# A float32 decoder trunk on one core: the FFN's last down group of three pairs by token block, the embedding's gate by token block, and other places for the first loads and the rotary tables

## The chip, the cores and the metric

The kernel runs on one core of a Trainium2 chip. The metric is the device time of the whole program in microseconds, as a median of several runs. The program computes two decoder layers on 512 tokens of 1024 features, all in float32. The core has five engines with queues of their own: TensorE (PE in the profile; its weight loads are PEld), VectorE (DVE), ScalarE (ACT), GpSimd (POOL) and SyncE (SP), which here issues the DMAs. Engines wait for each other by semaphores. Each engine takes its instructions in the order that was fixed when the program was built.

## The reference

Each layer runs four sub-layers, every one normalised before and after: a feed-forward network (FFN) at half weight, a token mixer, a second FFN, and a gated embedding. The mixer is retention with rotary positions in layer 0 and stick-breaking attention in layer 1.

```python
def swiglu(x, w_gate, w_up, w_down):
    return (jax.nn.silu(x @ w_gate) * (x @ w_up)) @ w_down

for i in range(DEPTH):
    g = norm_gains[i]
    f = swiglu(rmsnorm(h, g[0]), ffn_w_gate[i, 0], ffn_w_up[i, 0], ffn_w_down[i, 0])
    h = h + FFN_RES_WEIGHT * rmsnorm(f, g[1])
    m_in = rmsnorm(h, g[2])
    j = i // N_MIXERS
    if i % N_MIXERS == 0:
        m = retention(m_in, positions, ret_w_in[j], ret_gn_gain[j], ret_w_out[j])
    else:
        m = stick_breaking(m_in, sb_w_in[j], sb_w_out[j])
    h = h + rmsnorm(m, g[3])
    f = swiglu(rmsnorm(h, g[4]), ffn_w_gate[i, 1], ffn_w_up[i, 1], ffn_w_down[i, 1])
    h = h + FFN_RES_WEIGHT * rmsnorm(f, g[5])
    gate = jax.nn.sigmoid(rmsnorm(h, g[6]) @ ple_w_gate[i])
    e = p[i] @ ple_w_proj[i]
    h = h + rmsnorm(gate * e, g[7])
```

D_MODEL is 1024, D_FF is 2816, SEQ is 512, DEPTH is 2.

## The kernel before

**Split products.** Every float32 operand is split into a high part (a copy in the format fp32r, on ACT, line 154) and a low part (the difference, on DVE, line 151). A product is three multiplications: high by high, high by low and low by high (`mm3`, lines 159 to 161, and line 723 in the FFN). A weight tile comes by DMA into a raw buffer of 128 x 1024 (`_fetch`, line 208; eight buffers) and is split into a pair of buffers `wh`, `wl` (five pairs, `HL_BUFS`). Such a pair is called a unit here.

**The order of the weights.** `plan` lists all units in the order of their use. `_ahead` loads the next ones as long as a pair of buffers is free; `done_with` frees one. Some items have a home of their own instead (`home`): a place in a buffer that lies idle just then. It is opened by `open_home`. `bounds` stops loading four items into the next stage until `end_chain`. `gates` and `gated` tie the next loads behind given instructions: their ACT part and their DVE part are queued behind the named ones on the same engine.

**The FFN.** The 2816 hidden features are 22 blocks of 128, taken as 11 pairs. The first pair is computed plainly (`wstat_halves`: four units, first for tokens 0 to 255, then for the others). For each of the other ten pairs gate and up are computed with seven products instead of eight (`ORDER`, `gate_up`), each of 24 multiplications of 256 columns; sums of activation quarters (`xs`, four quarters; `xe`, three) and of weight quarters (line 245) feed them. Results are collected in `y` (lines 685, 686), pass Silu and the product with up (lines 740, 741) and are split into `hid` (`hidden`). Products 3 and 4 finish the two features of a pair.

The down projection is taken in groups of pairs (`GROUPS`). The steps of a group's down projection stand between the products of the next group (`ffn_steps`): one step takes one unit, 24 multiplications of 512 columns, over all four token blocks; a group's sums are added to `part`. The last group has no next one: its down projection is the FFN's tail.

**The tail and the chain.** `tail` goes token block by token block (128 tokens each): all units for block 0, then for block 1, and so on, so its units have to stay in place to the end. It has one or two halves of the output columns (`groups`). After each half `done` adds the sums to `part` (lines 556, 563) and does the sandwich normalisation: a square with a sum (522, 536), the product with the gain (526 on POOL, 537), the root (538, 539), the residual (544), then the next stage's own normalisation (458, 449, 450, 462). These steps of all blocks are tied to a fixed order on ACT, DVE and POOL (`chained`) and stand at high priority. Residual and square of block t run in the middle of block t+1 (`run_c`), the scaling (462) at its end (`run_d`). PE transposes the normalised blocks (468) at fixed points: block 0 behind tail block 2, block 1 in the middle of tail block 3, blocks 2 and 3 in the next stage (`flush`). The transposed blocks are split into `xs`, one half of it for tokens 0 to 255 and one for the others. The FFN's tail had the last group of two pairs: four units.

**The embedding.** `ple_e` computes p times its projection, then `ple` the gate in eight units: half 0 by `wmov` (unit after unit over all token blocks), half 1 by `tail`. `gated` multiplies the sigmoid (1195) with the embedding (1196).

**The order on the engines.** Where `traced` stands, PE takes its instructions as they are written. On the other engines the builder takes at each time the ready instruction of the best priority, by its own estimate of times. The rotary tables (`rope_tables`, lines 390 to 444) are written at step 20 of the first FFN and go to memory for retention.

```python
GROUPS = [(0, 1), (1, 4), (4, 7), (7, 9), (9, 11)]
ORDER = (1, 2, 6, 5, 7, 3, 4)
self.home.update({len(it) - 4: ("xe", 0), len(it) - 3: ("xe", 1), len(it) - 1: ("xe", 2)})
```

Of the kernel before, what the change touches and what calls it, by code (L numbers as in the profile page):

```python
# [25 lines left out]
NFB = FF // P  # L26
# [14 lines left out]
NTILES = 2 * DEPTH * 3 * NFB + 64 + 32 + 11 * DEPTH  # L41
GROUPS = [(0, 1), (1, 4), (4, 7), (7, 9), (9, 11)]
NHID = 16
# [4 lines left out]
def ffn_steps():  # L48

    out = [("gu", 1, 1), ("gu", 1, 2), ("down", 0, 0, 0), ("down", 0, 1, 0), ("gu", 2, 1), ("gu", 2, 2)]  # L50
    out += [("gu", p, prod) for p in (1, 2) for prod in ORDER[2:]]
    out += [("gu", 3, prod) for prod in ORDER]
    for g in range(2, len(GROUPS)):
        gu = [("gu", p, prod) for p in range(*GROUPS[g]) for prod in ORDER]
        down = [("down", g - 1, half, q) for half in range(2) for q in range(*GROUPS[g - 1])]
        at = [int((i + 0.7) * len(gu) / len(down)) for i in range(len(down))]
        at[-1] = len(gu) - 1
        for i, x in enumerate(gu):
            out.append(x)
            out += [d for d, a in zip(down, at) if a == i]  # L60
    return out
# [17 lines left out]
class Trunk:  # L79
# [69 lines left out]

    def low(self, eng, out, x, h):  # L150
        eng.tensor_tensor(out=out, in0=x, in1=h, op=ALU.subtract)  # L151

    def split(self, hl, x, eng=None):
        self.nc.scalar.activation(hl[0], x, AF.Copy)  # L154
        self.low(eng or self.nc.vector, hl[1], x, hl[0])

# [35 lines left out]
    def plain_specs(self, layer, j):  # L192
        return [(n, (layer, j), 0, NC, d * P, P) for d in range(2) for n in ("ffn_w_gate", "ffn_w_up")]

    def plan_ffn(self, layer, j):
        it = self.items
        it += [("w", x) for x in self.plain_specs(layer, j)]
        for x in ffn_steps():
            it.append(("st", (layer, j, x[1]), x[2]) if x[0] == "gu" else ("w", self.down_spec(layer, j, *x[2:])))
        g = len(GROUPS) - 1  # L200
        it += [("w", self.down_spec(layer, j, half, q)) for half in range(2) for q in range(*GROUPS[g])]

        self.home.update({len(it) - 4: ("xe", 0), len(it) - 3: ("xe", 1), len(it) - 1: ("xe", 2)})

# [23 lines left out]
    def piece(self, x, w, home=None):  # L228
        if home and home[0] == "blk":
            parts = [self.blk2() for _ in range(2)]  # L230
            for i, hl in enumerate(parts):
                self.split(hl, x[:, i * 512 : i * 512 + 512])
            return tuple(Parts(p) for p in zip(*parts))
        if home and home[0] == "xe":
            h, l = (self.xe[:, 2 * home[1] + i] for i in range(2))
        elif home:
            h, l = (self.work.tile([P, 1280], F32R, tag="pk", name="pk", bufs=self.npacks)[:, :w] for _ in range(2))
        else:
            h = self.hl.tile([P, 1024], F32R, tag="wh", name="wh")[:, :w]
            l = self.hl.tile([P, 1024], F32R, tag="wl", name="wl")[:, :w]  # L240
        self.split((h, l), x)
        return h, l
# [28 lines left out]
    def _ahead(self):  # L271
        while self.loaded < min([*self.bounds[:1], len(self.items)]):
# [6 lines left out]
            with ExitStack() as after:  # L279
                for ins in self.gates if self.gated else ():  # L280
                    after.enter_context(self.tc.issue_after(ins))
                self._load()
            self.gated = max(0, self.gated - 1)

# [398 lines left out]
    def ffn(self, layer, j, gpost, after, side=None):  # L683
# [9 lines left out]
        def hidden(f, u):  # L693
            hid[f] = self.blk2()
            self.split(hid[f], u)


# [16 lines left out]
        def gate_up(p, prod):  # L714
# [4 lines left out]
            for g in range(2):  # L719
                o = ps[:, g * 256 : g * 256 + 256]  # L720
                for k in range(4):
                    for n, (a, b) in enumerate(((0, 0), (0, 1), (1, 0))):
                        nc.tensor.matmul(o, w[a][:, g, k, :], x[b][:, k, :], start=new and g + k + n == 0,  # L723
                                         stop=k == 3 and n == 2, skip_group_check=True)
            self.done_with()

# [15 lines left out]

            if prod == 4:
                out(2, ps)
                hidden(2 * p, us.pop((p, 2 * p)))
            else:

# [4 lines left out]
                if prod == 3:  # L752
                    hidden(2 * p + 1, us.pop((p, 2 * p + 1)))

        def down(g, half, q):
# [19 lines left out]
        with self.traced():  # L775
            for n, x in enumerate(ffn_steps()):
                if n == 20 and side:
                    side()
                (gate_up if x[0] == "gu" else down)(*x[1:])
                if x[:2] == ("gu", NPAIR - 1) and x[2] in (6, 7, 3):  # L780
                    self.open_home(("xe", (6, 7, 3).index(x[2])))

# [407 lines left out]
    def ple(self, layer, e, gpost, after):  # L1190
# [8 lines left out]
        def done_a(t, ps):  # L1199
            gated(0, t, ps)  # L1200
            ssa[t] = self.post_a(t, gpost, False)

# [4 lines left out]

        specs = [[("ple_w_gate", (layer,), 256 * i, 2, half * 512, 512) for i in range(4)] for half in range(2)]
        self.open_home(*(("blk", i) for i in range(4)))
        self.wmov(specs[0], self.xstat, done_a)  # L1210
        self.tail(specs[1], lambda g, k, t: self.xstat(k, t), [range(4)], [done_b])


    def run(self):
# [13 lines left out]
        for t in range(NT):  # L1228
# [3 lines left out]
            if t == 1:  # L1232
                self.flush()
        self.layers()
        assert self.at == len(self.items), (self.at, len(self.items))
# [100 lines left out]
```

## Time and profile before

| what | value |
|---|---|
| median of 3 runs | 2239.42 us (2238.24 to 2240.11) |
| the profiled execution | 2239.47 us, span 2237.2 us |
| mean granted TensorE clock | 0.995 |
| first multiplication, last one's end (timeline) | 7.86 us, 2229.11 us |
| DVE, ACT, POOL busy | 66%, 45%, 10% |
| mean DMA | 111 GB/s |

The page of the profile gives busy times, the views of the trace give single instructions. A row of the timeline has the start from the beginning of the span, the duration, engine, line, operation, output and inputs with their shape, and in brackets the idle time of the engine just before with the one that ended it. A row of the waits names who waited for whom, with the total in us, the count and the longest. Matmuls are pipelined: a record is longer than the time from one start to the next.

### The profile page before, as it was taken

What the parts mean: (1) busy time and instruction counts of PE and PEld (TensorE: products, weight loads), DVE (VectorE), ACT (ScalarE), POOL (GpSimd) and SP (SyncE); (2) the same over time, 40 slices, a digit from 0 to 9 for tenths busy, and PEclk for the clock granted to TensorE, in tenths of its full rate; (3) what the DMA queues carried; (4) which work ended last, traced back from release to release, by engine and by line L of the source; (5) the groups of instructions that cost most, each with busy time, mean ns of one, the idle gap of its engine ahead of it and who ended that gap; (6) DMA issues with size and microseconds to landing.
All of it is one profiled execution on the core that took longest, in us unless ns stands there. A gap on an engine that the chain in (4) does not pass through costs nothing.

```text
span 2237.2 us, 33020 instructions
## 1 busy us (share of the span) xinstructions
PE 2175.6 (97%) x13640; PEld 1962.4 (88%) x13640; DVE 1476.6 (66%) x1739; ACT 1005.9 (45%) x1476; POOL 230.2 (10%) x337
## 2 busy tenths in 40 slices
PE   7899999999999999999999999999999999999998
PEld 7899998888888899999978999998988889999976
DVE  7977576553635588667665976666654569775764
ACT  5544344332223355444455544344555445443443
POOL 0000002110111210000023000002221220000022
PEclk9999999999999999999999999999999999999999
DMA  5332335321322324332453233335312232323351
GB/s 212 117 111 94 114 103 180 99 99 59 116 76 80 124 93 133 104 114 92 153 198 104 95 113 104 103 96 170 118 62 76 78 121 96 113 95 114 100 164 57
DMA packets 69414, 248.81 MB, mean 111 GB/s; under 512 B 7952, under 2 KB 7952, under 8 KB 69264
## 3 DMA queue, kind: packets, MB, share of 16 engines
q1 hardware_dynamic: 69264, 246.72, 33.4%
q8 instruction: 106, 1.74, 0.3%
q14 instruction: 44, 0.36, 0.0%
HBM read 229.38 MB, written 17.30 MB: 110 GB/s over the span
## 4 chain that ended last, share of the span: by engine, by line
PE 81%; DVE 9%; ACT 3%; POOL 3%; issue 2%; DMA 2%; DVEq 0%; SPq 0%; POOLq 0%; ACTq 0%
PE ps L723 31%; PE ps L160 16%; PE ps L161 16%; PE ps L159 16%; DMA raw<-wts 2%; DVE wl L151 2%; DVE part L544 1%; PE ps L1029 1%; DVE raw L245 1%; DVE xs L151 1%; ACT xn L458 1%; POOL st L539 1%; ACT junk L536 1%; DVE xn L462 1%; POOL st L538 1%
## 5 line engine op out<-in xcount | busy, mean ns | idle before, releaser
L151 DVE TENSOR_TENSOR wl<-raw,wh 128x1024 fp32r<-128x1024 f32 x435 | 537.3, 1238 | 389.6 <-ACT wh L154 387.0
L154 ACT ACTIVATE wh<-raw 128x1024 fp32r<-128x1024 f32 x435 | 459.8, 1060 | 692.4 <-PE ps L723 209.8
L723 PE MATMUL ps<-xs,wh 128*128 128x256 f32 x2560 | 463.7, 282 | 7.5 <-DVE y L685 7.5
L723 PEld LDWEIGHTS ps<-xs,wh 128*128 128x128 f32 x2560 | 398.6, 189 | 12.8 <-DVE y L685 9.1
L723 PE MATMUL ps<-xs,wl 128*128 128x256 f32 x1280 | 362.5, 283 | 0.0
L723 PE MATMUL ps<-xe,wh 128*128 128x256 f32 x1920 | 350.6, 284 | 0.0
L723 PEld LDWEIGHTS ps<-xe,wh 128*128 128x128 f32 x1920 | 302.1, 193 | 1.6
L159 PE MATMUL ps<-wh,blk 128*128 128x512 f32 x744 | 291.7, 392 | 1.9 <-ACT blk L154 1.9
L161 PE MATMUL ps<-wh,blk 128*128 128x512 f32 x744 | 290.7, 392 | 1.1 <-DVE blk L151 1.1
L160 PE MATMUL ps<-wl,blk 128*128 128x512 f32 x744 | 291.5, 392 | 0.0
L723 PE MATMUL ps<-xe,wl 128*128 128x256 f32 x960 | 272.8, 284 | 4.3 <-DVE wl L151 4.3
L723 PEld LDWEIGHTS ps<-xs,wl 128*128 128x128 f32 x1280 | 241.4, 189 | 0.0
L160 PE MATMUL ps<-xs,wh 128*128 128x256 f32 (+1 forms) x576 | 186.6, 324 | 4.9 <-DVE xs L151 4.7
L159 PE MATMUL ps<-xs,wh 128*128 128x256 f32 (+1 forms) x576 | 186.9, 324 | 2.1 <-ACT xs L154 2.0
L723 PEld LDWEIGHTS ps<-xe,wl 128*128 128x128 f32 x960 | 184.9, 193 | 4.5 <-DVE wl L151 4.5
L161 PE MATMUL ps<-xs,wl 128*128 128x256 f32 (+1 forms) x576 | 185.4, 322 | 0.0
L161 PEld LDWEIGHTS ps<-wh,blk 128*128 128x128 f32 x744 | 140.3, 189 | 31.4 <-DVE blk L151 1.5
L159 PEld LDWEIGHTS ps<-wh,blk 128*128 128x128 f32 x744 | 140.6, 189 | 29.5 <-ACT blk L154 2.1
L160 PEld LDWEIGHTS ps<-wl,blk 128*128 128x128 f32 x744 | 140.4, 189 | 27.2
L161 PE MATMUL ps<-wh,xs 128*128 128x512 f32 (+1 forms) x448 | 162.9, 364 | 0.0
L159 PE MATMUL ps<-wh,xs 128*128 128x512 f32 (+1 forms) x448 | 162.5, 363 | 0.0
L160 PE MATMUL ps<-wl,xs 128*128 128x512 f32 (+1 forms) x448 | 162.5, 363 | 0.0
(161 smaller groups left out, 3197.3 us busy)
## 6 DMA issues: line engine op xcount, KB each, us to landing
raw<-wts SPq DMA_DIRECT2D x382, 512.0 KB, 3.5
keep<-part SPq DMA_DIRECT2D x28, 512.0 KB, 4.3
rin<-keep SPq DMA_DIRECT2D x28, 512.0 KB, 4.2
gbc<-gains SPq DMA_DIRECT2D x16, 512.0 KB, 3.7
part<-x SPq DMA_DIRECT2D x4, 512.0 KB, 7.6
rin<-x SPq DMA_DIRECT2D x4, 512.0 KB, 4.3
out<-part SPq DMA_DIRECT2D x8, 256.0 KB, 2.2
dec<-decay SPq DMA_DIRECT2D x4, 256.0 KB, 3.7
```

What stands on the lines that cost most here:

```text
L151: eng.tensor_tensor(out=out, in0=x, in1=h, op=ALU.subtract)
L154: self.nc.scalar.activation(hl[0], x, AF.Copy)
L159: mm(ps, a[0], b[0], start=start, stop=False)
L160: mm(ps, a[0], b[1], start=False, stop=False)
L161: mm(ps, a[1], b[0], start=False, stop=stop)
L245: self.nc.vector.tensor_tensor(out=out, in0=a, in1=b, op=op)
L458: nc.scalar.activation(xn, self.part[t], AF.Square, scale=1.0 / 32, accum_out=ss)
L462: nc.vector.scalar_tensor_tensor(out=xn, in0=self.part[t], scalar=r, in1=g, op0=ALU.mult, op1=ALU.mult)
L536: nc.scalar.activation(self.junk, b, AF.Square, scale=k, accum_out=ss)
L538: nc.gpsimd.tensor_tensor(out=r, in0=ss, in1=ssa, op=ALU.add)
L539: nc.gpsimd.tensor_tensor(out=r, in0=r, in1=self.mhalf, op=ALU.pow)
L723: nc.tensor.matmul(o, w[a][:, g, k, :], x[b][:, k, :], start=new and g + k + n == 0, stop=k == 3 and n == 2, skip_group_check=True)
```

## The change

- `GROUPS` is cut as (0,1), (1,4), (4,6), (6,8), (8,11): the last group has three pairs, and the tail six units.
- In the steps of the last group the down steps are spread over all but the last three products; before, a group's last down step always stood behind its last product.
- The last five of the six tail units have homes: `xe` 0, `xs` 2, `xe` 1, `xe` 2, `xs` 3, opened behind products 6, 5, 7, 3 and 4 of the last pair.
- In the last pair the results are read at high priority; the buffers of products 3 and 4 are freed together behind the last product's reading; and behind the splits of each of the two last features the next three loads are tied (`gates`).
- At the start the loads of units 1 to 3 are tied behind the chain of token block 1.
- The rotary tables are written at step 50 instead of 20.
- The embedding's gate runs both halves in `tail`; the steps of half 0 are part of the chain.

```diff
-GROUPS = [(0, 1), (1, 4), (4, 7), (7, 9), (9, 11)]
+GROUPS = [(0, 1), (1, 4), (4, 6), (6, 8), (8, 11)]
...
-        at[-1] = len(gu) - 1
+        if g == len(GROUPS) - 1:
+
+            at = [int((i + 0.7) * (len(gu) - 3) / len(down)) for i in range(len(down))]
...
-    def low(self, eng, out, x, h):
-        eng.tensor_tensor(out=out, in0=x, in1=h, op=ALU.subtract)
-
-    def split(self, hl, x, eng=None):
-        self.nc.scalar.activation(hl[0], x, AF.Copy)
-        self.low(eng or self.nc.vector, hl[1], x, hl[0])
+    def split(self, hl, x):
+        h = self.nc.scalar.activation(hl[0], x, AF.Copy)
+        l = self.nc.vector.tensor_tensor(out=hl[1], in0=x, in1=hl[0], op=ALU.subtract)
+        self.split_ins = [h, l]
...
+    LAST = (("xe", 0), ("xs", 2), ("xe", 1), ("xe", 2), ("xs", 3))
...
-        self.home.update({len(it) - 4: ("xe", 0), len(it) - 3: ("xe", 1), len(it) - 1: ("xe", 2)})
+        self.home.update({len(it) - 5 + i: home for i, home in enumerate(self.LAST)})
...
-                for ins in self.gates if self.gated else ():
+                for ins in self.gates if self.gated and self.loaded else ():
                     after.enter_context(self.tc.issue_after(ins))
                 self._load()
-            self.gated = max(0, self.gated - 1)
+            self.gated = max(0, self.gated - (self.loaded > 1))
...
             self.split(hid[f], u)
+            if f >= NFB - 2:
+
+                self.gates, self.gated = [i.ins for i in self.split_ins], 3
...
-            self.done_with()
+            last = p == NPAIR - 1
+            if not (last and prod in ORDER[-2:]):
+                self.done_with()
...
+            with self.tc.high_priority(offset=HIGH) if last else nullcontext():
+                read()
+            if last and prod == ORDER[-1]:
+                self.done_with(2)
...
-                if n == 20 and side:
+                if n == 50 and side:
                     side()
                 (gate_up if x[0] == "gu" else down)(*x[1:])
-                if x[:2] == ("gu", NPAIR - 1) and x[2] in (6, 7, 3):
-                    self.open_home(("xe", (6, 7, 3).index(x[2])))
+                if x[:2] == ("gu", NPAIR - 1) and x[2] in ORDER[2:]:
+                    self.open_home(self.LAST[ORDER.index(x[2]) - 2])
...
         def done_a(t, ps):
-            gated(0, t, ps)
-            ssa[t] = self.post_a(t, gpost, False)
+            with self.chained():
+                gated(0, t, ps)
+                ssa[t] = self.post_a(t, gpost, False)
...
-        specs = [[("ple_w_gate", (layer,), 256 * i, 2, half * 512, 512) for i in range(4)] for half in range(2)]
+        specs = [("ple_w_gate", (layer,), 256 * i, 2, half * 512, 512) for half in range(2) for i in range(4)]
         self.open_home(*(("blk", i) for i in range(4)))
-        self.wmov(specs[0], self.xstat, done_a)
-        self.tail(specs[1], lambda g, k, t: self.xstat(k, t), [range(4)], [done_b])
+        self.tail(specs, lambda g, k, t: self.xstat(k, t), [range(4), range(4, 8)], [done_a, done_b])
...
             if t == 1:
                 self.flush()
+                self.gates, self.gated = list(self.ends.values()), 3
```

Where `gate_up` reads a product's results, the code is the same as before, now inside a function `read()`.

More of the change, by code (lines that the diff above doesn't have):

```diff
@@ L1 @@
 import math
-from contextlib import ExitStack, contextmanager
+from contextlib import ExitStack, contextmanager, nullcontext
 import numpy as np
@@ L233, in piece @@
             return tuple(Parts(p) for p in zip(*parts))
-        if home and home[0] == "xe":
-            h, l = (self.xe[:, 2 * home[1] + i] for i in range(2))
+        if home and home[0] in ("xe", "xs"):
+            h, l = (getattr(self, home[0])[:, 2 * home[1] + i] for i in range(2))
         elif home:
@@ L741, in out, with read @@
                 nc.vector.tensor_tensor(out=u, in0=u, in1=src[:, 256:], op=ALU.mult)
[L743 to L746, printed above, removed]
+            def read():
+                if prod == 4:
+                    out(2, ps)
+                    hidden(2 * p, us.pop((p, 2 * p)))
+                    return
                 n = {1: 0, 2: 0, 6: 1, 3: 1, 5: 3, 7: 3}[prod]
```

## The prediction

> **What bounds the kernel now.** I read the page's busy times first, then who TensorE waits for, over the whole span and stage by stage, then the timelines around those waits.
>
> ```profile
> span 2237.2 us, 33020 instructions
> ...
> PE 2175.6 (97%) x13640; PEld 1962.4 (88%) x13640; DVE 1476.6 (66%) x1739; ACT 1005.9 (45%) x1476; POOL 230.2 (10%) x337
> ```
> ```profile
> 101.29 31.70 PE ps L723 x264
> ```
> ```profile
> 348.57 0.40 PE L159 MATMUL ps<-wh,blk 128*128 128x512 f32 x1
> ...
> 353.83 0.39 PE L161 MATMUL ps<-wh,blk 128*128 128x512 f32 x1
> ```
>
> TensorE sets the time: 97% busy. In the chain of waits 264 multiplications of 256 columns take 31.70 us, 0.120 each; on PE's timeline the 24 of 512 columns of one down step start 23 intervals apart in 5.26 us, 0.229 each. A record lasts 0.39, so neighbours overlap by 0.16, and a wait costs 0.16 more than the idle time shown. The change leaves the count of multiplications alone, so it can only take away or add waits of PE. Where they are, by PE's own waits in four windows (the start; 354 to 395, first FFN into retention; 1112 to 1160, second FFN into the embedding; 1198 to 1226, embedding into the third FFN):
>
> ```profile
> PE ps L160 <- DVE xs L151: 2.2, 1, 2.2
> PE ps L159 <- ACT xs L154: 0.5, 1, 0.5
> ```
> ```profile
> PE ps L468 <- DVE xn L462: 2.1, 1, 2.1
> PE ps L160 <- DVE xs L151: 0.3, 1, 0.3
> PE ps L159 <- ACT xs L154: 0.2, 1, 0.2
> ```
> ```profile
> PE ps L468 <- DVE xn L462: 4.1, 3, 2.1
> ```
> ```profile
> PE ps L468 <- DVE xn L462: 3.0, 1, 3.0
> PE ps L160 <- DVE xs L151: 0.5, 2, 0.3
> ```
>
> The windows 1535 to 1600 (third FFN into attention) and 2138 to 2182 (fourth into the embedding) answer with the same rows as the second and the third. So each hand-over ends with PE waiting for the normalised block that it is to transpose (L462 to L468). Why, DVE's timeline shows (start, duration, what; in brackets the idle time before and who ended it):
>
> ```profile
> 358.34 0.69 DVE L563 TENSOR_TENSOR part<-part,ps 128x512 f32<-128x512 f32 x1 [1.12 <-PE ps L161]
> 359.88 0.69 DVE L537 TENSOR_TENSOR part<-part,gbc 128x512 f32<-128x512 f32 x1 [0.85 <-ACT junk L536]
> 361.28 1.28 DVE L544 SCALAR_TENSOR_TENSOR part<-part,st,rin 128x1024 f32<-128x1024 f32 x1 [0.71 <-POOL st L539]
> ...
> 368.27 1.29 DVE L544 SCALAR_TENSOR_TENSOR part<-part,st,rin 128x1024 f32<-128x1024 f32 x1 [0.44 <-POOL st L539]
> ...
> 372.15 1.48 DVE L537 TENSOR_TENSOR part<-part,gbc 128x512 f32<-128x512 f32 x1 [1.39 <-ACT junk L536]
> 373.55 1.27 DVE L462 SCALAR_TENSOR_TENSOR xn<-part,st,gbc 128x1024 f32<-128x1024 f32 x1
> ...
> 375.94 1.27 DVE L544 SCALAR_TENSOR_TENSOR part<-part,st,rin 128x1024 f32<-128x1024 f32 x1
> ```
>
> The chain has a fixed order, and from residual to residual (L544) it takes 7.0 us and then 7.7. PE works on a token block for 24 x 0.229 = 5.5. The chain falls some 2 us behind with each block, and before the fourth PE has no cover left.
>
> **The change part by part.** *Three pairs in the last down group.* A token block of the FFN's tail becomes 36 x 0.229 = 8.2 us, longer than the chain's 7.0 to 7.7, so the chain starts each block without arrears. From the first block, which had none: L563 starts at 358.34 and L537 ends at 360.57, 2.2 later; with L462 (1.27) 3.6 us after the block's last product. In the last block the transposes come after half a block, 18 x 0.229 = 4.1 us: 0.5 to spare, and the first block's transposes besides. After the tail the next transposes stand behind two units of 24 x 0.120 = 2.9 (mixer) or 24 x 0.229 = 5.5 us of embedding products, again later than 3.6; the two further waits into the embedding (2.0 together) come of the same arrears, since the work between those transposes stays. So the waits go: 2.1 + 0.3 + 0.2 + 3 x 0.16 = 3.1 into each mixer, 4.1 + 3 x 0.16 = 4.6 into each embedding, together **-15.4**. Next late would be the halves for the first multiplication of the next stage, which get half a block of 4.1 us behind the transposes instead of 2.7. The new homes of the weights (quarters of the transposed activations) are rewritten only by blocks 2 and 3 of the next stage, behind the whole tail in PE's own order.
>
> *No down step behind the last products.* Today one (5.5 us) covers the reading of the last feature pair. Its rows, from the last product on PE through ACT and DVE:
>
> ```profile
> 348.45 0.28 PE L723 MATMUL ps<-xs,wl 128*128 128x256 f32 x1
> ```
> ```profile
> 348.70 1.06 ACT L154 ACTIVATE wh<-raw 128x1024 fp32r<-128x1024 f32 x1 [0.54 <-ACT u L740]
> 349.66 0.37 ACT L740 ACTIVATE u<-ps 128x256 f32<-128x256 f32 x1
> ...
> 351.38 0.63 ACT L154 ACTIVATE blk<-u 128x512 fp32r<-128x512 f32 x1 [0.83 <-DVE u L741]
> ```
> ```profile
> 349.79 1.23 DVE L151 TENSOR_TENSOR wl<-raw,wh 128x1024 fp32r<-128x1024 f32 x1 [0.16 <-ACT wh L154]
> 350.93 0.42 DVE L741 TENSOR_TENSOR u<-u,ps 128x256 f32<-128x256 f32 x1
> ...
> 352.82 0.69 DVE L151 TENSOR_TENSOR blk<-u,blk 128x512 fp32r<-128x512 f32 x1
> ```
>
> The low half is ready at 353.51, 5.1 us after the last product's start, with loads (1.06, 1.23) in between; the four steps alone are 0.37 + 0.42 + 0.63 + 0.69 = 2.1. After the change the tail first multiplies the four earlier features (12 x 0.229) and two terms of this one: 3.2 us of cover. High priority and the tie keep loads away, except one tied to feature 21 alone, which stands ready when ACT and DVE are free. Bounds 0 (steps alone) and 5.1 - 3.2 = 1.9; I take the middle, 0.9, for four FFNs **+3.6**. Behind the tie wait the tail's last two units and then the next stage's four, six ACT copies of 1.06 and DVE parts of 1.23 (7.4); the first block's 8.2 us hide them. Without that cover the last unit alone would cost 1.06 + 1.23 = 2.3.
>
> *The gate by token block.* Its tail block grows from 5.5 to 10.9 us, far above the chain's 7.7: 3.0 + 0.3 + 2 x 0.16 go at the embedding's hand-over, **-3.6**. The last embedding has no PE wait, and the chain from its last product to the output is the same work: 0. But the eight gate units, used over 44 us before (5.5 each), are all wanted in the first 10.9, at 1.37 each. DVE's part, from the grouped view of 1155 to 1170:
>
> ```profile
> L151 DVE TENSOR_TENSOR wl<-raw,wh 128x1024 fp32r<-128x1024 f32 x5 | 6.0, 1223 | 0.7 <-ACT wh L154 0.4
> ...
> L151 DVE TENSOR_TENSOR blk<-raw,blk 128x512 fp32r<-128x512 f32 x8 | 5.1, 684 | 0.0
> ```
>
> Four of the five and all eight halves are the gate's: 10.4 us, 1.30 a unit, just PE's rate. What else lands on DVE there (a unit of the next stage, 1.22, a product of the chain, 0.69) PE waits for: 0 to 1.9, I take 0.6, twice **+1.2**. The next FFN's first units load during the last block, when the gate's buffers come free: three DVE parts of 1.23 beside a chain of at most 7.7 in 10.9: 3.7 + 7.7 = 11.4, half a microsecond over if DVE were busy for all of the chain, which it isn't (the idle times in the rows above): 0.
>
> *The start.* DVE's timeline:
>
> ```profile
> 12.14 1.28 DVE L151 TENSOR_TENSOR xs<-ps,xs 128x512 fp32r<-128x512 f32 x2
> 13.34 2.35 DVE L151 TENSOR_TENSOR wl<-raw,wh 128x1024 fp32r<-128x1024 f32 x2
> 15.61 1.28 DVE L151 TENSOR_TENSOR xs<-ps,xs 128x512 fp32r<-128x512 f32 x2
> ```
>
> Two weight parts (2.35) stand ahead of the second block's halves. Tied behind them they go later, where their units are wanted 2.9 us apart: **-2.0** (0 to -2.4). From the windows view:
>
> ```profile
> 16.35:21.42 5.07, 5.07 (x23) 5.07 (x24) 4.06 (x4) 1.06 (x1) 0.76 (x3) 1.00 1.02 416
> ```
>
> Here 23 multiplications take 5.07 us, 0.22 each instead of 0.120, although the granted clock reads 1.00. [...]
>
> *The rotary tables.* Their rows by tile, and one of the DMA queue:
>
> ```profile
> L408 DVE SCALAR_TENSOR_TENSOR rope<-rope x10: 682/683/693, 32.0 to 76.8; 128x512 f32<-128x512 f32 x10
> ...
> L442 ACT ACTIVATE rope<-rope x1: 617/617/617, 85.7 to 85.7; 128x512 f32<-128x512 f32 x1
> ```
> ```profile
> 15.02 0.43 SPq L513 DMA_DIRECT2D rin<-x  x1
> ```
>
> Step 20 is the sixth of the eleven products in the row of 264, at about 116 us; the tables ran from before 32 to 86. The residual's load, written in the tail (from 354), was issued at 15. So the order takes work as early as its buffers allow, and at step 50 the tables will run where they run now: **0**.
>
> Sum: -15.4 + 3.6 - 3.6 + 1.2 - 2.0 = -16.2. The profiled run took 2239.47 (span 2237.2 and 2.3 around it), the median is 2239.42: **2223**.
>
> **The rivals.** *The tables do move* out of the first FFN, whose DVE is full. In the first FFN PE waits once where later FFNs don't:
>
> ```profile
> PE ps L723 <- DVE wl L151: 4.3, 1, 4.3
> ```
> ```profile
> 71.00:75.20 4.20, 4.19 (x19) 4.20 (x20) 4.20 (x6) 0.00 (x0) 0.00 (x0) 0.50 0.15 54
> ```
>
> That wait (4.5) and the half clock behind it (0.50; 19 multiplications in 4.2 instead of 2.3 us) would go: -6.4, 2217. Against it stands the row at 15.02.
>
> *The hand-overs stay half.* The chain keeps to its own 7 us and meets extra loads; 8.2 is only 0.5 above 7.7. Half of 19.0 stays: 2233.
>
> *The last features are uncovered.* Today six multiplications of the tail run ahead of the last two products:
>
> ```profile
> 341.46 0.40 PE L159 MATMUL ps<-xe,blk 128*128 128x512 f32 x1
> ...
> 342.62 0.39 PE L161 MATMUL ps<-xe,blk 128*128 128x512 f32 x1
> ```
>
> If all twelve do, the cover falls from 3.2 to 0.5, and the wait to as much as 4.6; at 4.0 in each FFN 2223 - 3.6 + 16 = 2236. For it speaks the 5.1 of today, against it the high priority.
>
> *Slower: the tied loads come on the path.* Place: the first tail block of each FFN. Besides the lost cover (4.6) PE would wait for three tied units, 3 x 1.23 = 3.7: 8.3 an FFN, 2223 - 3.6 + 33 = 2252. It outweighs the gains (21.0 - 1.2) from 5.0 us an FFN on. Against it: the last unit is wanted 6.9 us into the block.
>
> **How the numbers follow.** Forecast 2223 (own range 2218 to 2229) 0.55; tables move 0.11; half hand-overs 0.13; features uncovered 0.15, around 2236 on both sides of the border; slower 0.06. About 0.2% (4.5 us) is what a measurement of this kernel can tell from no change, so faster is below 2235: 0.55 + 0.11 + 0.12 + 0.06 = 0.84; same 0.10; slower 0.06. The range 2214 to 2235 takes in the first three cases and the nearer part of the fourth.
>
> **What would show it.** Right: L468 no longer waits for L462 at the five hand-overs; residuals 8.2 us apart in FFN tails and 10.9 in the gate's; the first low-half wait gone; tables again between 26 and 90 us. Wrong: an idle time of PE over 1 us between L723 and the first tail products, waits for weights in the gate's first block, or L468's rows still there.

## The result and the profile after

| kernel | median, us | lowest to highest | runs |
|---|---|---|---|
| before | 2239.11 | 2238.24 to 2240.11 | 4 |
| changed | 2220.43 | 2219.31 to 2220.81 | 4 |

The ratio is 0.9911 with a 95% interval of 0.9899 to 0.9923: 18.7 us less, clear of no change. The profiled execution of the changed kernel took 2220.81 us. Its page (span and busy times):

```profile
span 2218.9 us, 32989 instructions
...
PE 2174.7 (98%) x13640; PEld 1962.7 (88%) x13640; DVE 1466.0 (66%) x1739; ACT 1003.4 (45%) x1476; POOL 236.7 (11%) x337
```

TensorE has the same 13640 multiplications, busy for 1 us less, in a span that is 18.3 us shorter: nothing was made cheaper, waits went. Line numbers after the diff are higher: 154 and 153 (low and high part) for 151 and 154, 464 and 470 for 462 and 468, 687 for 685, 728 for 723, 747 and 748 for 740 and 741, 539, 546 and 565 for 537, 544 and 563. PE's waits over the whole span (total, count, longest):

```profile
PE ps L470 <- DVE xn L464: 15.0, 4, 8.1
PE ps L728 <- DVE y L687: 6.6, 5, 2.5
PE ps L728 <- DVE wl L154: 4.3, 1, 4.3
PE ps L159 <- ACT blk L153: 3.5, 5, 1.9
```

The four waits left in the first row are two at the start (9.3, the longest 8.1) and two at the end of attention (5.7). None is left behind an FFN or between the embedding and the next FFN. Before the change that row held 13 waits and 28.7 us. DVE's timeline in the first FFN's tail shows the chain in its new rhythm:

```profile
351.67 1.28 DVE L546 SCALAR_TENSOR_TENSOR part<-part,st,rin 128x1024 f32<-128x1024 f32 x1 [0.71 <-POOL st L541]
...
355.91 0.69 DVE L565 TENSOR_TENSOR part<-part,ps 128x512 f32<-128x512 f32 x1 [2.36 <-PE ps L161]
...
359.78 1.29 DVE L546 SCALAR_TENSOR_TENSOR part<-part,st,rin 128x1024 f32<-128x1024 f32 x1 [0.44 <-POOL st L541]
```

These two residuals (L546) are 8.1 us apart, and DVE waits 2.36 us for the block's product (L565): the chain is ahead of TensorE. The next two come 8.9 and 9.4 us later, where transposes (1.04 us for a block) stand between TensorE's products. In the gate the residuals, from 1162.27 on, are 12.1, 11.8 and 12.6 us apart. The 10.9 of the forecast counted the products alone: it left out the transposes before the last block and the scaling of the block before (L464, 1.28), which stands ahead of the second residual.

TensorE does the same work in both kernels, so its start times can be compared at equal shares of that work (columns multiplied so far, counted along PE's timelines of the two profiled executions). The changed kernel less the kernel before, and the pieces between:

| share of PE's work | shift, us | piece | forecast |
|---|---|---|---|
| 14%, first FFN | -3.4 | start: -3.4 | -2.0 |
| 18%, retention | -5.7 | first FFN's end: -2.3 | -2.2 |
| 50%, second FFN | -6.6 | retention and the FFN: -0.9 | 0 |
| 54%, embedding | -10.0 | second FFN's end: -3.4 | -3.7 |
| 56%, third FFN | -14.0 | embedding's end: -4.0 | -3.0 |
| 68%, third FFN | -13.5 | +0.5 | 0 |
| 72%, attention | -15.8 | third FFN's end: -2.3 | -2.2 |
| 84%, fourth FFN | -17.6 | attention and its end: -1.7 | 0 |
| 94%, fourth FFN | -14.5 | +3.1 | 0 |
| 98%, embedding | -18.3 | fourth FFN's end: -3.8 | -3.7 |
| 100% | -18.3 | 0 | +0.6 |

### The profile page after: what moved, and what is told of

Read it like the earlier page. It is cut to its first block, busy times and chain, and to the rows that moved or that the text cites. A ratio compares the mean times of both kernels' runs of the same rounds, so it can differ in the third digit from the quotient of the medians.

```text
span 2218.9 us, 32989 instructions
## 1 busy us (share of the span) xinstructions
PE 2174.7 (98%) x13640; PEld 1962.7 (88%) x13640; DVE 1466.0 (66%) x1739; ACT 1003.4 (45%) x1476; POOL 236.7 (11%) x337
## 4 chain that ended last, share of the span: by engine, by line
PE 88%; DVE 6%; ACT 2%; issue 1%; POOL 1%; DMA 1%; SPq 0%; DVEq 0%; POOLq 0%; ACTq 0%
PE ps L728 33%; PE ps L160 18%; PE ps L159 18%; PE ps L161 18%; PE ps L1042 1%; DVE wl L154 1%; DMA raw<-wts 1%; DVE raw L247 1%; DVE xs L154 1%; PE ps L470 1%; DVE part L546 0%; DVE xe L154 0%; DVE y L687 0%; ACT xn L460 0%; POOL st L541 0%
## 5 line engine op out<-in xcount | busy, mean ns | idle before, releaser
L154 DVE TENSOR_TENSOR wl<-raw,wh 128x1024 fp32r<-128x1024 f32 x427 | 526.6, 1239 | 356.2 <-ACT wh L153 353.5
L153 ACT ACTIVATE wh<-raw 128x1024 fp32r<-128x1024 f32 x427 | 449.8, 1059 | 640.5 <-PE ps L728 202.2
L159 PE MATMUL ps<-wh,blk 128*128 128x512 f32 x680 | 266.3, 392 | 1.9 <-ACT blk L153 1.9
L161 PE MATMUL ps<-wh,blk 128*128 128x512 f32 x680 | 265.2, 391 | 1.1 <-DVE blk L154 1.1
L160 PE MATMUL ps<-wl,blk 128*128 128x512 f32 x680 | 266.0, 391 | 0.0
L159 PE MATMUL ps<-xs,wh 128*128 128x256 f32 (+1 forms) x576 | 186.5, 324 | 0.2 <-ACT xs L153 0.2
L159 PE MATMUL ps<-wh,xs 128*128 128x512 f32 (+1 forms) x448 | 162.7, 363 | 0.0
L526 POOL TENSOR_SCALAR st<-st 128x1 f32<-128x1 f32 x32 | 8.9, 279 | 1375.0 <-ACT junk L524 1358.9
L161 PEld LDWEIGHTS ps<-wh,blk 128*128 128x128 f32 x680 | 128.0, 188 | 28.7 <-DVE blk L154 1.5
L159 PEld LDWEIGHTS ps<-wh,blk 128*128 128x128 f32 x680 | 128.2, 189 | 26.8 <-ACT blk L153 2.1
```

Source lines behind the costliest of these rows:

```text
L153: h = self.nc.scalar.activation(hl[0], x, AF.Copy)
L154: l = self.nc.vector.tensor_tensor(out=hl[1], in0=x, in1=hl[0], op=ALU.subtract)
L159: mm(ps, a[0], b[0], start=start, stop=False)
L160: mm(ps, a[0], b[1], start=False, stop=False)
L161: mm(ps, a[1], b[0], start=False, stop=stop)
L526: nc.gpsimd.tensor_scalar(out=r, in0=ss, scalar1=1.0, scalar2=(4 if half else 1) * RMS_EPS, op0=ALU.mult, op1=ALU.add)
```

## The experiments

Times of all of them (the kernel before, run beside each on the same chip, had medians of 2239.0 to 2240.4 us; a ratio is to those runs, with its 95% interval):

| experiment | median, us | ratio |
|---|---|---|
| two pairs in the last group | 2254.61 | 1.0070 (1.0055 to 1.0085) |
| no tie, no priority, early freeing | 2241.88 | 1.0013 (1.0003 to 1.0022) |
| no tie | 2241.09 | 1.0013 (1.0003 to 1.0022) |
| tie behind feature 21 alone | 2245.69 | 1.0020 (1.0010 to 1.0029) |
| tie behind feature 20 alone | 2216.22 | 0.9887 (0.9872 to 0.9902) |
| gate's half 0 unit by unit | 2224.70 | 0.9933 (0.9918 to 0.9948) |
| start untied | 2221.00 | 0.9922 (0.9910 to 0.9935) |
| tables tied | 2212.70 | 0.9879 (0.9863 to 0.9896) |
| kernel before, tables tied | 2232.14 | 0.9970 (0.9958 to 0.9982) |
| tables tied, start untied | 2214.31 | 0.9882 (0.9867 to 0.9897) |
| tables tied, tie behind feature 20 alone | 2210.52 | 0.9877 (0.9861 to 0.9893) |

**Two pairs again in the last group.** Everything else is as changed.

```diff
-GROUPS = [(0, 1), (1, 4), (4, 6), (6, 8), (8, 11)]
+GROUPS = [(0, 1), (1, 4), (4, 7), (7, 9), (9, 11)]
...
-        self.home.update({len(it) - 5 + i: home for i, home in enumerate(self.LAST)})
+        self.home.update({len(it) - 4: ("xe", 0), len(it) - 3: ("xe", 1), len(it) - 1: ("xe", 2)})
```

> The changed kernel with the groups and the homes of before: the last down group has two pairs again, tie, priority and the rest stay. Theory (the hand-overs waited because a tail block of 24 x 0.229 = 5.5 us is shorter than the chain's 7.0 to 7.7): DVE's normalisation ends PE's wait again at all four FFN hand-overs, 2.1 us into each mixer and some 4.1 in three waits into each embedding, +15.4 us; the last features have 6 multiplications of cover instead of 12, +1.4 in each FFN: about 2241. Rival (the ties and the priority keep DVE free for the chain, block length matters little): hand-over waits stay under 1 us each, only the features cost, about 2226.

Measured: 2254.61, far above. PE's waits:

```profile
PE ps L470 <- DVE xn L464: 27.6, 12, 8.2
PE ps L159 <- ACT blk L153: 16.3, 5, 3.6
```

The first row is what was to be shown: the waits at the FFNs' ends are back with the shorter blocks (12 waits and 27.6 us, against 4 and 15.0 in the changed kernel). The second row was not expected in this size: 3.6 us for the last feature in every FFN. PE's and DVE's timelines and the windows view around it:

```profile
353.78 0.80 PE L159 MATMUL ps<-xe,blk 128*128 128x512 f32 x1 [3.59 <-ACT blk L153]
```
```profile
350.38 2.35 DVE L154 TENSOR_TENSOR wl<-raw,wh 128x1024 fp32r<-128x1024 f32 x2
352.65 0.41 DVE L748 TENSOR_TENSOR u<-u,ps 128x256 f32<-128x256 f32 x1
353.76 0.69 DVE L154 TENSOR_TENSOR blk<-u,blk 128x512 fp32r<-128x512 f32 x1 [0.69 <-ACT blk L153]
```
```profile
354.00:360.00 6.00, 6.00 (x16) 4.61 (x17) 3.40 (x4) 2.35 (x4) 1.43 (x2) 0.54 0.80 273
```

Two weight parts (2.35) stand on DVE between the product and the reading of its result (L748). The windows row has the stretch, its length, the busy time of PE, PEld, DVE, ACT and POOL with the counts, the granted clock, the DMA share and GB/s: behind the wait the clock is 0.54, with 16 multiplications in 6 us. So loads among the reading's steps, and the clock behind the wait, are the price to look for.

**The reading of the last features: neither tie nor priority.** The three edits that protect it are taken out.

```diff
-            if f >= NFB - 2:
-                self.gates, self.gated = [i.ins for i in self.split_ins], 3
...
-            if not (last and prod in ORDER[-2:]):
-                self.done_with()
+            self.done_with()
...
-            with self.tc.high_priority(offset=HIGH) if last else nullcontext():
-                read()
-            if last and prod == ORDER[-1]:
-                self.done_with(2)
+            read()
```

> The changed kernel without the tie behind the last features, without the high priority of the last pair's reading and without the common release of its last two buffers; three pairs stay. Theory: the hand-overs keep no wait, since the block length is unchanged; only the wait before the last features' first tail product grows from 0.55 us in each FFN to at most 1.9: 2220.4 to 2226. Rival (tie and priority made the gain): the waits for the normalised block come back, 2.1 and 4.1, 2236.

Measured: 2241.88. The waits at the FFNs' ends stay gone (first row, over the whole span), so it is the length of the blocks that removed them. But the whole gain is given back at the last features. PE's waits from 325 to 360, DVE's timeline (L744 is the step that is L748 in the changed kernel), and the windows view:

```profile
PE ps L470 <- DVE xn L464: 13.5, 4, 8.1
...
PE ps L159 <- ACT blk L153: 2.9, 1, 2.9
PE ps L161 <- DVE blk L154: 0.5, 1, 0.5
```
```profile
342.32 1.23 DVE L154 TENSOR_TENSOR wl<-raw,wh 128x1024 fp32r<-128x1024 f32 x1 [0.16 <-ACT wh L153]
343.46 0.41 DVE L744 TENSOR_TENSOR u<-u,ps 128x256 f32<-128x256 f32 x1
343.79 1.22 DVE L154 TENSOR_TENSOR xs<-raw,xs 128x1024 fp32r<-128x1024 f32 x1
344.93 1.28 DVE L154 TENSOR_TENSOR blk<-u,blk 128x512 fp32r<-128x512 f32 x2
```
```profile
345.00:350.00 5.00, 4.49 (x11) 2.99 (x11) 1.90 (x4) 0.72 (x2) 0.09 (x1) 0.50 0.71 236
```

Two things come together. Two loads (wl and xs, 1.22 each) stand among the four steps of the reading. And ten of the tail's twelve covering multiplications now stand ahead of the last two products in TensorE's order (333.08 to 335.54), so only two (0.46) are left as cover behind them. In all it costs 21.5 us over the changed kernel, at equal work 5.3 to 6.2 in each FFN: some 3 by the longer waits, the rest by the half clock behind them, at which 11 multiplications of 512 columns take 5 us where 22 fit at 0.229. Had the eight multiplications that ran ahead stayed behind (8 x 0.229 = 1.8), the wait of 2.86 would have been about 1.0, an estimate; that part is the loads'.

**Which of the three does it.** First the tie alone is taken out.

```diff
-            if f >= NFB - 2:
-                self.gates, self.gated = [i.ins for i in self.split_ins], 3
```

> The changed kernel without the tie of three loads behind each of the two last features; high priority and the late freeing of the two last buffers stay. Theory (the tie alone keeps the tail's multiplications and the loads behind the reading of the last features): PE waits for the last feature 4 to 5 us in each of four FFNs with half clock behind it, as in the kernel without tie, priority and late freeing, and the time is 2238 to 2244. Rival (the late freeing of the two buffers already keeps the loads away from the reading): the waits are below 1 us each, and the time is within 3 us of the changed kernel's, 2219 to 2224. In between, 2226 to 2235, each carries a part. What high priority does by itself needs no run: without it the built program has the same order on every engine.

Measured: 2241.09, with the same waits for the last feature as above (13.4 us in the row of L159 behind blk, 2.9 the longest). The traces of this kernel and of the one above have the same instructions in the same order on every engine. So without the tie neither the late freeing of the two buffers nor the high priority moves anything, and the tie makes all of the 21; with the tie in place, no run leaves out one of the other two.

Does the tie work by the cover or by the loads? Each of its two halves is taken alone:

```diff
-            if f >= NFB - 2:
+            if f == NFB - 1:
```

> The changed kernel, with three loads tied only behind the feature that is read first (21), none behind the one read last (20). The built order shows: TensorE's order is that of the changed kernel, ten multiplications of the tail behind the last product, but four weight copies (1.06 each on ACT, 1.22 on DVE) and one of a quarter now stand ahead of the reading of feature 20. Theory (loads among the reading's steps make the wait, whatever the cover): the wait for the last feature grows from 0.4 to 4 to 6 us in each FFN, with half clock behind it, and the time is 2236 to 2248. Rival (cover decides: with ten multiplications behind the last product the loads are hidden): the waits stay below 1 us, 2219 to 2223.

Measured: 2245.69. The waits (the row holds one more, of 1.9 in attention) and DVE's timeline of the first FFN:

```profile
PE ps L159 <- ACT blk L153: 21.6, 5, 4.9
```
```profile
339.29 1.23 DVE L154 TENSOR_TENSOR xe<-raw,xe 128x1024 fp32r<-128x1024 f32 x1 [0.26 <-ACT xe L153]
340.43 4.62 DVE L154 TENSOR_TENSOR wl<-raw,wh 128x1024 fp32r<-128x1024 f32 x4
344.98 0.41 DVE L748 TENSOR_TENSOR u<-u,ps 128x256 f32<-128x256 f32 x1
345.31 1.22 DVE L154 TENSOR_TENSOR xs<-raw,xs 128x1024 fp32r<-128x1024 f32 x1
346.44 0.68 DVE L154 TENSOR_TENSOR blk<-u,blk 128x512 fp32r<-128x512 f32 x1
```

TensorE's order is that of the changed kernel, with ten multiplications of cover. It still waits 4.9 us, because five loads (the first two rows, 5.8 us together) stand on DVE ahead of the reading's step (L748, 344.98); a sixth stands between it and the low half. Then the other half alone:

```diff
-            if f >= NFB - 2:
+            if f == NFB - 2:
```

> The changed kernel, with three loads tied only behind the feature that is read last (20). The built order shows: TensorE's order as in the changed kernel; one load of a quarter (1.06 on ACT, 1.22 on DVE) stands ahead of the steps of feature 21, none among those of feature 20. Theory (only loads ahead of the last feature's own four steps count): the waits stay at 0.4 to 0.6 us, and the time is within 2 us of the changed kernel's 2220.4. Rival (the load ahead of feature 21 pushes both features): the waits are 1.5 to 2 us, and the time is 2225 to 2228.

Measured: 2216.22, less than the changed kernel by more than either theory had. DVE's timeline of the changed kernel, and of this one:

```profile
339.25 1.23 DVE L154 TENSOR_TENSOR xe<-raw,xe 128x1024 fp32r<-128x1024 f32 x1 [0.26 <-ACT xe L153]
340.40 0.42 DVE L748 TENSOR_TENSOR u<-u,ps 128x256 f32<-128x256 f32 x1
341.51 0.69 DVE L154 TENSOR_TENSOR blk<-u,blk 128x512 fp32r<-128x512 f32 x1 [0.70 <-ACT blk L153]
```
```profile
336.69 1.23 DVE L154 TENSOR_TENSOR xe<-raw,xe 128x1024 fp32r<-128x1024 f32 x1 [0.40 <-ACT xe L153]
337.83 0.42 DVE L748 TENSOR_TENSOR u<-u,y 128x256 f32<-128x256 f32 x1
338.86 0.42 DVE L748 TENSOR_TENSOR u<-u,ps 128x256 f32<-128x256 f32 x1 [0.62 <-ACT u L747]
339.38 1.29 DVE L154 TENSOR_TENSOR blk<-u,blk 128x512 fp32r<-128x512 f32 x2
```

In the changed kernel one load, tied to feature 21 alone, stands ahead of the last reading (339.25), and TensorE waits 0.39. With the tie behind feature 20 alone that load comes while the last product still runs (336.69), both halves are ready at 340.67, and the four waits are gone. They cost more than the idle time shows. PE's timeline of the changed kernel behind the wait:

```profile
341.53 0.50 PE L159 MATMUL ps<-xs,blk 128*128 128x512 f32 x1 [0.39 <-ACT blk L153]
341.87 0.40 PE L160 MATMUL ps<-xs,blk 128*128 128x512 f32 x1
342.26 0.50 PE L161 MATMUL ps<-xs,blk 128*128 128x512 f32 x1
342.60 0.39 PE L159 MATMUL ps<-xs,blk 128*128 128x512 f32 x1
```

The wait is 0.39 + 0.16 = 0.55, and the next starts are 0.34, 0.39 and 0.34 apart instead of 0.23, the second of them because the low half is ready only at 342.20. At equal work the kernel with the tie behind feature 20 gains 0.92 to 0.96 there in each FFN, 3.7 together. By the traces (span 2214.1 for 2218.9) another 1.6 goes in the fourth FFN ahead of its end, where the clock stayed full (1.00, last section), and 0.5 is lost elsewhere. The five kernels in one table, from their timelines of the first FFN:

| kernel | loads that start on DVE between the last product's last multiplication and the low half | tail multiplications behind it | first wait |
|---|---|---|---|
| tie behind 20 alone | 0 | 10 | none |
| changed | 1 | 10 | 0.39 |
| no tie, no priority | 2 | 2 | 2.86 |
| two pairs | 3 | 3 | 3.59 |
| tie behind 21 alone | 6 | 10 | 4.93 |

**The gate's half 0 unit by unit** as before the change:

```diff
-            with self.chained():
-                gated(0, t, ps)
-                ssa[t] = self.post_a(t, gpost, False)
+            gated(0, t, ps)
+            ssa[t] = self.post_a(t, gpost, False)
...
-        self.tail(specs, lambda g, k, t: self.xstat(k, t), [range(4), range(4, 8)], [done_a, done_b])
+        self.wmov(specs[0], self.xstat, done_a)
+        self.tail(specs[1], lambda g, k, t: self.xstat(k, t), [range(4)], [done_b])
```

> The changed kernel with the embedding's gate as before: half 0 unit after unit over all token blocks, half 1 by token block of 5.5 us. Theory: the first embedding's hand-over waits again, 3.0 + 0.3 and the overlap, +3.6 to +4.0: 2224.4; nothing at the last embedding. Rival (in its first block the gate waits for its weights, which gives the gain back): 2220 to 2221.

Measured: 2224.70, 4.3 more than changed. The wait at the embedding's end is back, here from 1195 to 1225:

```profile
PE ps L470 <- DVE xn L464: 3.0, 1, 3.0
```

At equal work this kernel loses 3.7 us against the changed one between 50% and 56%, where the gate lies; its other pieces, up to 2.1 us each way, add up to 0.2. In the changed kernel PE waits for nothing from 1140 to 1197, so the gate's eight units in one block cost nothing there.

**The start untied.**

```diff
-                self.gates, self.gated = list(self.ends.values()), 3
```

> The changed kernel without the tie at the start (the loads of units 1 to 3 are no longer queued behind the chain of token block 1); everything else is as changed. Theory (the early shift of the changed kernel, 3.4 us by 4% of TensorE's work, comes from the two weight parts of 1.2 us that no longer stand between the first and the second block's halves on DVE): the first low half comes 2.1 us later (16.35 instead of 14.25), the wait L160 for the low half of about 2.2 us is back, and the time is 2.1 to 3.4 us longer than that of the changed kernel, 2222.5 to 2224. Rival (the early shift comes from elsewhere, the order of the whole DVE queue in the first FFN): the wait is back, but by 4% of the work the kernel has lost nothing against the changed one, and the time is within 1 us of it.

Measured: 2221.00, 0.6 more than changed, which the runs can't tell from nothing. The wait (0 to 30) is back, though, and against the changed kernel this one is 2.4 us late at 14% of the work. The changed kernel and then this one:

```profile
PE ps L160 <- DVE xs L154: 0.5, 1, 0.5
```
```profile
PE ps L160 <- DVE xs L154: 2.3, 1, 2.3
```

So the place does give its 2.4. The rest of the 3.4 in the table is in the first FFN: from 90 to 110 us PE waits 1.3 for y in the kernel before, 0.4 in this one and not at all in the changed one. It is the fourth FFN that evens it out. The changed kernel's DVE timeline and windows there:

```profile
1869.18 1.23 DVE L247 TENSOR_TENSOR t<-raw 128x1024 f32<-128x1024 f32 x1 [2.27 <-DMA raw<-wts]
...
1873.80 1.22 DVE L154 TENSOR_TENSOR wl<-raw,wh 128x1024 fp32r<-128x1024 f32 x1
1874.94 0.68 DVE L687 TENSOR_TENSOR y<-y,ps 128x512 f32<-128x512 f32 x1
```
```profile
1875.70:1880.00 4.30, 4.30 (x24) 4.30 (x25) 4.30 (x6) 0.79 (x2) 0.00 (x0) 0.61 0.00 0
```

DVE waits 2.27 us for a weight tile from memory, makes up the queue behind it, and reads y (L687) late; TensorE waits 2.5 us and then runs at a granted clock of 0.61. Without the tie at the start the same place has waits of 1.3 and 0.5 and a clock of 1.00. A kernel that has no such stretch decides:

```diff
-                self.gates, self.gated = list(self.ends.values()), 3
...
                 if n == 50 and side:
-                    side()
+                    with self.tc.issue_after(self.split_ins[0].ins), self.tc.issue_after(self.split_ins[1].ins):
+                        side()
```

> The kernel with the rotary tables tied (2212.7), and without the tie of the first loads at the start. Theory (the tie at the start is worth the 2.4 to 2.7 us that the early multiplications show; without it the changed kernel got them back only because its fourth FFN no longer had a wait of 2.5 us with half clock behind it, and the kernel with tied tables has no such wait there): the shift of 2.4 to 2.7 us stays to the end, 2215 to 2215.5. Rival (the place is given back in any case, since a later wait for weights from memory ends at a time of its own): within 1 us of 2212.7.

Measured: 2214.31 against 2212.70 with the tie, spans 2211.9 and 2210.0: between the two expectations. It starts 2.6 late and keeps 1.9 of that to the end. The ratios alone (0.9882 and 0.9879, their intervals overlap) don't show a difference; the two traces do.

**The rotary tables.** Written at step 20 their main row ran from 32.0 to 76.8 us, written at step 50 it runs from 30.1 to 74.9: the later place did not move them, though no run has that edit alone. Tied behind the last feature split by then, they do move:

```diff
                 if n == 50 and side:
-                    side()
+                    with self.tc.issue_after(self.split_ins[0].ins), self.tc.issue_after(self.split_ins[1].ins):
+                        side()
```

> The changed kernel with the rotary tables tied, on ACT and DVE, behind the last weight split that was written before step 50, so that they cannot run earlier. Theory (the tables, some 13 us of DVE in the first FFN's full stretch, cause PE's wait of 4.3 us at 64.5 and the half clock behind it): both go, tables run at 200 us or later and cost nothing there, -6.4: 2214. Rival (DVE is as full there without them, by the sums of quarters): the wait stays above 3 us, 2219 to 2221.

Measured: 2212.70, 7.7 below the changed kernel. The tables' main row by tile and the window 65 to 70, in the changed kernel and in this one:

```profile
L410 DVE SCALAR_TENSOR_TENSOR rope<-rope x10: 686/694/706, 30.1 to 74.9; 128x512 f32<-128x512 f32 x10
```
```profile
65.00:70.00 5.00, 0.91 (x4) 0.91 (x5) 5.00 (x7) 2.31 (x4) 0.00 (x0) 0.76 0.00 0
```
```profile
L410 DVE SCALAR_TENSOR_TENSOR rope<-rope x10: 681/684/693, 224.8 to 256.9; 128x512 f32<-128x512 f32 x10
```
```profile
65.00:70.00 5.00, 5.00 (x44) 5.00 (x43) 4.21 (x6) 3.34 (x5) 0.00 (x0) 1.00 0.77 243
```

Where TensorE had 4 multiplications in 5 us it has 44. At equal work 6.9 us are gained by 4% of the work, behind the tables' old place. The span is 8.9 shorter: 2.8 more is the loss in the fourth FFN, which does not come here, and 0.8 is lost elsewhere. The same edit on the kernel before (whose `split` gets the two instructions as a list):

```diff
-                if n == 20 and side:
-                    side()
+                if n == 50 and side:
+                    with self.tc.issue_after(self.split_ins[0].ins), self.tc.issue_after(self.split_ins[1].ins):
+                        side()
```

> The kernel before, with the rotary tables written at step 50 and tied behind the splits of the last feature that was written by then, and nothing else changed. Theory (the tables that run in the first FFN's full DVE queue make the wait for wl of 4.3 us at 66.7 and the half clock behind it, in the kernel before as in the changed one): the wait and the half clock at 71 to 75 are gone, and the time is 6 to 8 us below the kernel before, 2231.5 to 2233.5. Rival (that wait has another cause, and the tables tied in the changed kernel gained by a change of the whole order): the wait stays, and the time is within 2 us of the kernel before.

Measured: 2232.14, 7.0 below the kernel before, and PE waits for nothing from 60 to 76. The 4.3 us wait was the tables' in both kernels. At equal work this kernel is 7.7 us ahead at 4% and 8.7 at 50%. By the end 2.0 of that is lost again, by the author's estimate to half clock at other places: the mean granted clock is 0.995 as in the kernel before, although the clock from 71 to 75.2 is 1.00 here and 0.50 there.

**Both edits that helped**, the tables tied and the tie behind feature 20 alone:

```diff
-            if f >= NFB - 2:
+            if f == NFB - 2:
...
-                    side()
+                    with self.tc.issue_after(self.split_ins[0].ins), self.tc.issue_after(self.split_ins[1].ins):
+                        side()
```

> The changed kernel with both edits that made it shorter: the rotary tables tied behind the last feature that was split by step 50, and three loads tied only behind the feature read last. Theory (they act at different places, the tables at 64 to 75 us and the loads at the end of each FFN): the four waits for the last feature of 0.55 each go from 2212.7, and the time is 2210 to 2211. Rival (the places of the queues in the FFNs shift, and a wait for y with half clock behind it comes back in one of them): 2212 to 2215.

Measured: 2210.52, as by the theory: 9.9 below the changed kernel and 28.5 below the one before. It is the lowest median, but the times alone don't tell it from the kernel with the tables tied (ratios 0.9877 and 0.9879). In the traces the four waits for the last feature are gone, and the span is 2208.1 instead of 2210.0.

## Why the prediction was right

Forecast 2223 with a range of 2214 to 2235; measured 2220.4. Point by point:

- **Hand-overs and last features, -15.4 + 3.6 = -11.8.** The four pieces of the table add up to -11.8. The mechanism is as told: the blocks became longer than the chain, and with shorter blocks every wait at the FFNs' ends came back. The last features cost 0.9 each (3.7 together, by the kernel with the tie behind feature 20), so the hand-overs alone gave 15.5. That the middle of the bounds was met so closely is luck: the working gave no reason for the middle, one load less among the reading's steps makes the wait 0, and five more make it 4.9.
- **The bounds of the last features hold only with the tie.** The upper end, 1.9 = 5.1 - 3.2, took the cover of 3.2 us for granted (in the changed kernel it is ten multiplications, 2.3) and left out the clock behind a wait, which the prediction itself had used for the tables. Without the tie the waits are 3.4 (2.9 + 0.5) and the loss is some 5.2 an FFN (20.7 in four). The rival with uncovered features (2236) was thus a real one. The multiplications that it named do run ahead, ten of twelve, and the loads among the reading's steps are the other part. The high priority that was named against it does nothing without the tie; the tie alone stood between the forecast and 2241. The one load "tied to feature 21 alone" that the prediction let through is indeed the one that made the 0.39.
- **The gate, -3.6 + 1.2.** The hand-over gave 4.0, though the 0.3 for the first halves did not go: PE's waits for them are 0.5 in two in both kernels. The 1.2 for a race of the eight weights wasn't there: PE waits for nothing in the first embedding's tail (1140 to 1197) nor in the second's (2150 to 2202). The 0.6 for each gate was too much; no run shows at which rate of loading such a loss would begin.
- **The start, -2.0.** The first low half comes 2.1 earlier, and 1.9 of it is left at 2% of the work; the tie gives 2.4 by the untied run. The 3.4 of the table has the wait for y in it, which the forecast did not have. The slow stretch itself hardly changed (23 multiplications in 5.05 us, before 5.07).
- **The tables, 0.** Right, and the rows fit the reason that was given, an order that takes them as early as their buffers allow: they run where they ran. The rival that they move would have been worth 6.9 in the changed kernel and 7.7 in the one before by 4% of the work, not 6.4.
- **Half hand-overs** (2233) didn't come: not one such wait is left. **Slower by tied loads** (2252) didn't come at its place, the first tail block. The tie behind feature 21 alone shows the price of loads in front of TensorE, 4.9 us in each FFN and, in the first, a clock of 0.66 behind it from 346 to 351 (2245.7 in all), but among the steps of the reading, not in the block.
- **Not forecast:** -0.9 in retention and the second FFN, -1.7 in attention and the early fourth FFN, +3.1 in the fourth FFN, +0.5 in the third: +1.0 together. The +3.1 is the late weight tile with the low clock behind it, shown above in the trace. What sets the arrival of that tile is open. The tie behind feature 20 alone has the same wait there (2.5) and loses 1.6 less, since the clock stayed full behind it (1.00).

So the forecast was 2.1 us too high by the traces (a gain of 16.2, measured 18.3): the start by 1.4, the gate by 1.0 and its last block by 0.6, while the 1.0 not forecast went the other way. The cause was right; that the time came so near is in part luck, since pieces of up to 3.1 us that the forecast did not have nearly cancelled.

## What to carry to other kernels

When a fixed chain of other engines follows each block of TensorE's work, compare the block's length with the chain's period: here a block that was half a microsecond longer removed the waits, and a shorter one made them grow from block to block. Before TensorE's last product of a phase is read, count the loads that stand among the reading's steps on each engine and the independent multiplications that stand behind that product; both are fixed in the built order, and a tie behind the last reading step moves both. Writing low-urgency work later in the program may not move it at all; look where it runs in the trace, and tie it if it is in the way. The last section gives a reason to compare stages at equal work and not totals alone.

## What the runs showed of the hardware

The granted clock falls to a half behind some waits of TensorE, and not by their length alone. It was 0.61 behind a wait of 2.5 us in the fourth FFN of the changed kernel, and 1.00 behind the same wait with the tie behind feature 20 alone. Behind the wait of 3.0 us at the embedding's end in the kernel before it was 1.00 (1203.5 to 1208). At the end of attention in the changed kernel it was 1.00 behind a wait of 3.5 us (1789.3 to 1794) and 0.66 behind the next one, of 2.2 us (1794 to 1799). Two windows of the fourth FFN, in the changed kernel and then with the tie behind feature 20 alone:

```profile
1873.23:1876.64 3.41, 0.97 (x8) 0.97 (x9) 3.41 (x4) 1.44 (x3) 0.00 (x0) 1.00 0.00 0
1876.64:1880.06 3.42, 3.42 (x19) 3.42 (x18) 3.42 (x6) 0.42 (x1) 0.00 (x0) 0.50 0.00 0
```
```profile
1871.76:1875.17 3.41, 1.85 (x15) 1.85 (x16) 3.41 (x5) 0.69 (x3) 0.00 (x0) 1.00 0.00 0
1875.17:1878.59 3.42, 3.42 (x31) 3.42 (x30) 3.42 (x5) 2.23 (x4) 0.00 (x0) 1.00 0.00 0
```

TensorE is idle for 2.44 of the 3.41 us of the first row in the changed kernel, and has 19 multiplications in the 3.42 us behind it. With the tie behind feature 20 alone it is idle for 1.56 of 3.41 us, and has 31 in the 3.42 us behind it. What in a wait decides between the two was not shown.

Between 30 us and the last multiplication the clock is 0.50 from 69.30 to 76.12, 1775.96 to 1782.79 and 1806.68 to 1810.09 in the kernel before, and from 67.58 to 74.41, 1760.59 to 1764.00, 1794.72 to 1798.14 and 1876.64 to 1880.06 in the changed one. So such a stretch lasted some 3.4 or 6.8 us, and it costs up to 1.7 or 3.4 us where TensorE is busy all through it, an estimate (half of its length). Since the same wait of 2.5 us had half clock behind it in one kernel and full clock in another, sums of waits of 2 to 4 us are uncertain by a few microseconds however well the waits are known.
